# Strassen's scheme for part of the first up projection, with the S5 tables built in one batch

## The chip, the cores and the metric

The kernel runs on one core of one Trainium2 chip. The metric is the device time of one execution in microseconds (us). The kernel before takes 966.59 us, the median of 3 runs (966.46 to 968.69).

The core has a matrix engine (TensorE, PE in the profile, with its weight loads shown apart as PEld), VectorE (DVE), ScalarE (ACT), GpSimd (POOL), and SyncE (SP), whose queue issues nearly all DMA transfers here. Each engine works off its own queue in order.

## What the reference computes

One decoder layer on 512 tokens of width 1024, in float32, with adaLN shifts, scales and gates from a vector c:

```python
h = modulate(x, sh1, sc1)
x = layer_norm(ALPHA * x + 0.5 * g1 * swiglu(h, ffn1_w1, ffn1_w3, ffn1_w2), ...)
h = modulate(x, sh2, sc2)
m = hybrid_mixer(h, ...)          # Mamba-2 SSD heads and S5 heads, one shared w_in and w_out
x = layer_norm(ALPHA * x + g2 * m, ...)
h = modulate(x, sh3, sc3)
x = layer_norm(ALPHA * x + 0.5 * g3 * swiglu(h, ffn2_w1, ffn2_w3, ffn2_w2), ...)
# swiglu(u, w1, w3, w2) = (silu(u @ w1) * (u @ w3)) @ w2, inner width D_FF = 2816
# mod = (silu(c) @ w_ada + b_ada), nine chunks of 1024: shift, scale, gate three times
```

S5 is a complex diagonal state space with 32 groups of 64 states and 16 channels. Its discretised A, its B and its C depend on parameters only, not on the tokens.

## The kernel before, in words

**Arithmetic.** PE multiplies in the type fp32r. Each operand is split into a high part (a cast on ACT, `whi`) and the rest (a subtraction on DVE, `wlo`), and `mm3` (L101) makes each product of three matmuls: hi x hi, hi x lo, lo x hi.

**Stages.** The trace shows, in order: the first adaLN chunks with early pieces of the up projection (0 to 54 us), the first up projection (54 to 258), the first down projection (258 to 396), the mixer (396 to 607), the second up projection with its plain head (607 to 683) and its Strassen part (683 to 843), and the second down projection (843 to 967).

**Up projection.** The 2816 inner columns are 22 blocks f of 128. For each f, `up` (L397) multiplies the block of w1 (j = 0) and of w3 (j = 1) with all 512 tokens: 8 depth blocks x 3 matmuls of 512 columns each. `glue` (L384) then makes silu(a) * b on ACT and DVE into a tile `g`; the 22 blocks live in 11 `g` tiles. In the second projection `up_fast` (L477) takes the last 16 blocks by Strassen's scheme in Winograd's form: two blocks f, f+1 of one weight matrix form a 2 x 2 partition with the depth halves, the tokens another, and seven products replace eight. Each product is 4 depth blocks x 3 matmuls of 256 columns. A unit needs four sums of weights (L511, L512, L514, L522), all on DVE in before; the sums of the activations are made once by `h_sums` (L439).

**Side jobs.** Work that is not a projection is written as generators, and `step` (L609) advances them by a number of steps at places inside the projections. `s5_setup` (L775) builds, from parameters, four quarters b of tables: powers of A (`E`, seven doublings per real and imaginary part by `cmul`, six DVE operations each), the products `P0..P3` of B and `Q0..Q3` of C with powers of A. ACT copies P into block-diagonal tiles `bd` (L857), PE transposes them (L870) and multiplies them with `cd` (L901), and each quarter leaves for DRAM through tiles with tag `s5mp`, of which there are two (five uses a quarter, L872 to L919). The adaLN chunks are `ada_gate` (L302) and `ada_pair` (L283): each chunk is eight 512 KB loads into two `ra` buffers and eight DVE accumulates into `acc` (L276, L278). In `body` the side jobs of the first up projection are s5_setup with 4 steps per f, and from f = 11 the adaLN jobs with 3 steps per f; the down projection then advances the adaLN jobs by one step per f and half, and `L.step(ada, 1000)` finishes what is left:

```python
ada = [xres(), L.ada_gate(2, 0.5, g1), L.ada_pair(3, m2), L.ada_pair(6, m3), L.ada_gate(5, 1.0, g2)]
L.up(hT, gp, g, f0, jobs, 4, late=(ada, 3, 11), done=pss[f0, 0])
...
L.down(NF, getl_of(g, gl), L.make_drain(res, lambda: g1[0], ln1), 6, ada, 1)
L.step(ada, 1000)
```

xres yields 4 times, a gate 11 times (8 accumulates, 3 more), a pair 22 times.

**What sets the order.** The program is written once, engine by engine in the order of the calls; a scheduler then places the instructions in the engines' queues and may move ready work of ACT, DVE and the DMA queues ahead of work that comes earlier in the program. At run time each queue is strictly in order, and waits go by semaphores.

**Drains.** At the end of a down projection `make_drain` (L656) takes each of the four token tiles from PSUM: two or three DVE operations, bn_stats, a square root on POOL, the normalisation, and then `to_h` (L330) transposes it on PE and splits it for the next stage. The mixer begins with the z projection, whose weights are split as `zw`.

## Time and profile before

| | before |
|---|---|
| median of 3 runs | 966.59 us (966.46 to 968.69) |
| the profiled execution | 968.27 us, span 966.6 us |
| PE busy | 944.9 us, 5409 matmuls |
| DVE busy | 758.4 us, 1522 instructions |
| ACT busy | 446.9 us, 879 instructions |
| POOL busy | 34.2 us, 73 instructions |

The span is the time from the first to the last instruction of one profiled execution; 1.7 us of that execution's time lie around it. A share is busy time by span. The chain that ended last is followed back from the last instruction: at each step to what released it, or to the instruction before it on its engine; its shares say which engine's work the end depends on. Matmuls overlap in PE's pipeline, so the time of one is the distance from its start to the next one's, not the duration in its row.

### The profile page before, as it was taken

To read this page: it belongs to the slowest core of one execution; us is meant where nothing else is said; L and a number is where in the kernel's file an instruction comes from. 1 tells how busy PE (TensorE), PEld (TensorE's weight loads), DVE (VectorE), ACT (ScalarE), POOL (GpSimd) and SP (SyncE) were. 2 spreads that over 40 slices of the span, in tenths; PEclk is the share of its full clock that TensorE was granted. 3 is DMA by queue.
4 is the path that set the end of the run, shared out by engine and by line. 5 is a ranking of instruction groups with operands and counts; after the bars stand their busy time and mean duration, and the time that the engine had idled before them with its cause. 6 is when DMAs were issued, how large, how long until landed. Compare 5 with 4: busy or idle time off the path is not lost.

```text
span 966.6 us, 14710 instructions
## 1 busy us (share of the span) xinstructions
PE 944.9 (98%) x5409; PEld 798.1 (83%) x5409; DVE 758.4 (78%) x1522; ACT 446.9 (46%) x879; POOL 34.2 (4%) x73
## 2 busy tenths in 40 slices
...
GB/s 342 377 190 270 188 280 162 157 174 122 261 204 197 242 217 180 86 233 71 142 121 67 1 88 152 173 111 66 88 99 120 89 129 90 175 152 109 109 1 87
DMA packets 75578, 147.93 MB, mean 153 GB/s; under 512 B 11633, under 2 KB 28657, under 8 KB 74993
## 3 DMA queue, kind: packets, MB, share of 16 engines
...
q14 instruction: 32, 0.25, 0.1%
...
## 4 chain that ended last, share of the span: by engine, by line
PE 86%; DVE 6%; ACT 4%; issue 2%; POOL 1%; DMA 0%; DVEq 0%; POOLq 0%; ACTq 0%
PE ps L103 27%; PE ps L104 27%; PE ps L105 27%; DVE cv L90 1%; PE ps L253 1%; PE ps L978 1%; DVE wlo L81 1%; PE ps L207 1%; ACT whi L96 1%; POOL rsx L170 1%; DVE s5X L81 0%; DMA raw<-in_w_in_dram 0%; PE ps L295 0%; DVE s5t L81 0%; PE ps L949 0%
## 5 line engine op out<-in xcount | busy, mean ns | idle before, releaser
L96 ACT CAST whi<-raw 128x1024 fp32r<-128x1024 f32 (+1 forms) x155 | 155.0, 1007 | 211.5 <-PE ps L104 97.5
L81 DVE TENSOR_TENSOR wlo<-raw,whi 128x1024 fp32r<-128x1024 f32 (+1 forms) x155 | 179.3, 1167 | 43.0 <-ACT whi L96 42.5
L103 PE MATMUL ps<-hT,whi 128*128 128x512 f32 x448 | 177.0, 396 | 1.7 <-ACT hT L1492 1.7
L104 PE MATMUL ps<-hT,whi 128*128 128x512 f32 x448 | 174.7, 390 | 0.1
L105 PE MATMUL ps<-hT,wlo 128*128 128x512 f32 x448 | 174.6, 390 | 0.0
L103 PE MATMUL ps<-whi,ghl 128*128 128x512 f32 x320 | 125.2, 391 | 0.0
L104 PE MATMUL ps<-wlo,ghl 128*128 128x512 f32 x320 | 124.5, 389 | 0.0
L105 PE MATMUL ps<-whi,ghl 128*128 128x512 f32 x320 | 124.3, 389 | 0.0
L103 PEld LDWEIGHTS ps<-hT,whi 128*128 128x128 f32 x448 | 83.9, 188 | 23.3 <-issue 3.2
L105 PEld LDWEIGHTS ps<-hT,wlo 128*128 128x128 f32 x448 | 84.1, 188 | 17.8
L104 PEld LDWEIGHTS ps<-hT,whi 128*128 128x128 f32 x448 | 84.2, 188 | 17.0 <-DVE hT L81 0.5
L103 PE MATMUL ps<-hx,whi 128*128 128x256 f32 (+1 forms) x320 | 97.5, 305 | 0.7 <-DVE cp L90 0.6
L104 PE MATMUL ps<-hx,whi 128*128 128x256 f32 (+1 forms) x320 | 97.3, 304 | 0.0
L105 PE MATMUL ps<-hx,wlo 128*128 128x256 f32 (+1 forms) x320 | 97.3, 304 | 0.0
L90 DVE SCALAR_TENSOR_TENSOR acc<-ra,cs,acc 128x1024 f32<-128x1024 f32 (+2 forms) x62 | 71.0, 1145 | 22.4 <-DMA ra<-in_w_ada_dram 21.9
L96 ACT CAST ghl<-g 128x512 fp32r<-128x512 f32 x88 | 53.1, 619 | 50.1 <-PE ps L105 37.5
L103 PEld LDWEIGHTS ps<-whi,ghl 128*128 128x128 f32 x320 | 60.1, 188 | 14.6 <-issue 2.5
L105 PEld LDWEIGHTS ps<-whi,ghl 128*128 128x128 f32 x320 | 60.1, 188 | 12.6
L104 PEld LDWEIGHTS ps<-wlo,ghl 128*128 128x128 f32 x320 | 60.1, 188 | 12.3
L81 DVE TENSOR_TENSOR ghl<-g,ghl 128x512 fp32r<-128x512 f32 x88 | 58.1, 686 | 13.6 <-ACT ghl L96 13.6
L103 PEld LDWEIGHTS ps<-hx,whi 128*128 128x128 f32 x320 | 61.1, 191 | 3.9 <-issue 0.8
L104 PEld LDWEIGHTS ps<-hx,whi 128*128 128x128 f32 x320 | 61.2, 191 | 2.6
...
## 6 DMA issues: line engine op xcount, KB each, us to landing
ra<-in_w_ada_dram SPq DMA_DIRECT2D x56, 512.0 KB, 4.5
raw<-in_up_dram SPq DMA_DIRECT2D x49, 512.0 KB, 4.2
raw<-in_ffn_w_dram SPq DMA_DIRECT2D x44, 512.0 KB, 4.4
raw<-in_up_dram SPq DMA_DIRECT2D x64, 256.0 KB, 3.8
ra<-in_ada_dram SPq DMA_DIRECT2D x16, 512.0 KB, 7.8
raw<-in_w_in_dram SPq DMA_DIRECT2D x16, 512.0 KB, 4.4
s5d<-s5mp SPq DMA_DIRECT2D x20, 256.0 KB, 3.8
...
```

The lines of the kernel that those rows point to most:

```text
L81: self.nc.vector.tensor_tensor(out=out, in0=a, in1=b, op=op)
L90: self.nc.vector.scalar_tensor_tensor(out=out, in0=a, scalar=s, in1=b, op0=op0, op1=op1, **k)
L96: keep(self.nc.scalar.copy(out=hi, in_=src))
L103: mm(o, lh, rh, start=first, stop=False, **k)
L104: mm(o, lh, rl, start=False, stop=False, **k)
L105: self.last_mm = mm(o, ll, rh, start=False, stop=last, **k)
L170: self.nc.gpsimd.tensor_scalar(out=x, in0=var, scalar1=EPS, scalar2=None, op0=ADD)
L207: self.nc.tensor.matmul(ps, self.onesr, bc(self.onesr, (1, 4)), start=True, stop=True)
L253: nc.tensor.matmul(bank[q:q + 32, 0:256], lhs, w[:, :, m * P:(m + 1) * P], start=(j < 2), stop=(j >= len(put) - 2))
L978: nc.tensor.matmul(pv[32 * r:32 * r + 32, j, :], M[:, n, r, 32 * j:32 * j + 32], rhs[:, r, :], start=(n == 0), stop=(n == 2))
```

## The change

Four things change:

- The first up projection now takes its blocks f = 14 to 21 by `up_fast`, that is 8 units (4 pairs f, f+1, times j). Blocks 12 and 13 are plain and carry `h_sums`. In these units (add=True) two of the four weight sums are made by DMA transfers issued on POOL that add into their destination: one adds a weight block from DRAM to a raw tile just loaded, one adds a half of the sum tile `c` to a raw tile in SBUF.
- In the second up projection the plain head shrinks from 6 to 4 blocks (FAST 6 to 4), so 2 more units go by Strassen's scheme.
- `s5_setup` is batched: E is made in two halves of two quarters, with operations up to 512 wide, P and Q for all four quarters at once with 256-wide operations. Their scratch are the five last `g` tiles of the projection (`L.spare`). After that the four quarters' copies, transposes and transfers follow one another. It is stepped 6 times per f instead of 4.
- The adaLN jobs get 2 steps per f from f = 10 up to f = 11, then 2 steps per unit in `up_fast`, then one per f and half in the down projection, where the unfinished tail of `up_fast` (one step) stands ahead of them. The down projection's weights and those behind are put in the queue by `down1()` in the last unit.

```diff
-    def up_fast(self, hq, new, gp, gts, g, w, f0, last, jobs):
+    def up_fast(self, v, new, c, sp, gp, g, w, f0, last, jobs, per, add=False):
...
+            if add:
+                x = ts[0][:, 512:1024].rearrange("p (k n) -> p k n", k=4)
+                nc.gpsimd.dma_start(out=x, in_=w[f][:, j, 0:4], accum_op=ADD)
...
         def prep_a(u):
             a, b = raws[u]
-            self.tt(c[:, lo_], a[:, hi_], b[:, hi_], ADD)
-            self.tt(a[:, hi_], a[:, hi_], a[:, lo_], ADD)
+            if not add:
+                self.tt(c[:, lo_], a[:, hi_], b[:, hi_], ADD)
+                self.tt(a[:, hi_], a[:, hi_], a[:, lo_], ADD)
             split(u, a, ("b11", "t1"))
             self.tt(c[:, hi_], a[:, hi_], b[:, hi_], ADD)
+            if add:
+                self.tt(c[:, lo_], c[:, hi_], a[:, lo_], SUB)
 
         def prep_b(u):
-            split(u, raws[u][1], ("b21", "b22"))
+            b = raws[u][1]
+            split(u, b, ("b21", "b22"))
+            if add:
+                nc.gpsimd.dma_start(out=b[:, lo_], in_=c[:, hi_], accum_op=ADD)
 
         def prep_c(u):
             split(u, c, ("t3", "t2"))
-            b = raws[u][1]
-            self.tt(b[:, lo_], b[:, lo_], c[:, hi_], ADD)
+            if not add:
+                b = raws[u][1]
+                self.tt(b[:, lo_], b[:, lo_], c[:, hi_], ADD)
...
-            self.step(jobs, 1)
+            self.step(jobs, per)
...
-        E = (pt("Er", [P, 4, P]), pt("Ei", [P, 4, P]))
-        w3 = [P, 4, 16]
-        Pk = [(pt(f"p{k}r", w3), pt(f"p{k}i", w3)) for k in range(4)]
-        Qk = [(pt(f"q{k}r", w3), pt(f"q{k}i", w3)) for k in range(4)]
-        u1, u2 = pt("s5u1", w3), pt("s5u2", w3)
+
+        xt = big[4].rearrange("p a (q n) -> p a q n", n=64)
+        for h in range(2):
+            E = [big[2 * n + h].rearrange("p a (q t) -> p (a q) t", t=P) for n in range(2)]
+            q = slice(8 * h, 8 * h + 8)
+            nc.vector.memset(E[0][:, :, 0:1], 1.0)
+            nc.vector.memset(E[1][:, :, 0:1], 0.0)
+            for lg in range(7):
+                n = 1 << lg
+                er, ei = en[lg]
+                self.cmul(E[0][:, :, n:2 * n], E[1][:, :, n:2 * n], bc(er[:, q], (2, n)), bc(ei[:, q], (2, n)),
+                          E[0][:, :, 0:n], E[1][:, :, 0:n], xt[:, 0, :, :n], xt[:, 1, :, :n])
+                if lg in (3, 5):
+                    yield
+            for b in range(2):
+                for n in range(2):
+                    nc.sync.dma_start(out=self.s5_dram[2 * h + b][:, 2 + n], in_=E[n][:, 4 * b:4 * b + 4])
+            yield
+        v4 = lambda t: t.rearrange("p a (c q h) -> p (a c) q h", c=2, h=16)
+        PQ = [v4(t) for t in big[:4]]
+        Pk = [(PQ[k // 2][:, 2 * (k % 2)], PQ[k // 2][:, 2 * (k % 2) + 1]) for k in range(4)]
+        Qk = [(PQ[2 + k // 2][:, 2 * (k % 2)], PQ[2 + k // 2][:, 2 * (k % 2) + 1]) for k in range(4)]
+        u = v4(big[4])
+        u1, u2 = u[:, 0], u[:, 1]
+        wb = lambda a: bc(a, (2, 16))
+        self.cmul(*Pk[0], wb(fr), wb(fi), bt['s5_b_re'], bt['s5_b_im'], u1, u2)
+        yield
+        for k in (1, 2, 3):
+            self.cmul(*Pk[k], wb(A[k][0]), wb(A[k][1]), *Pk[0], u1, u2)
+            yield
+        for j in range(4):
+            self.cmul(*Qk[j], wb(A[j + 1][0]), wb(A[j + 1][1]), cb['s5_c_re'], cb['s5_c_im'], u1, u2)
+            yield
...
-            self.cmul(*Pk[0], wb(fr), wb(fi), bt['s5_b_re'][:, q], bt['s5_b_im'][:, q], u1, u2)
-            for k in (1, 2, 3):
-                if k == 2:
-                    yield
-                self.cmul(*Pk[k], wb(A[k][0]), wb(A[k][1]), *Pk[0], u1, u2)
...
-                        nc.scalar.copy(out=bd[n][sl, :, 3 - k, g, :], in_=Pk[k][n][sl])
+                        nc.scalar.copy(out=bd[n][sl, :, 3 - k, g, :], in_=Pk[k][n][sl, q])
...
-        FAST = 6
+        FAST1 = 14
+        FAST = 4
...
+        wsum = [L.gates.tile([P, 1024], F32, tag="gate", bufs=2, name="wsum1")]
+
+        def down1():
+            L.want_down(NF, ins['ffn1_w2'][0])
+            L.wlimit = len(L.wq)
+            L.want_mixer()
+            L.want_up(ins['up2'], (), HALVES, g_alloc, FAST)
+            L.wahead(L.wi + 2)
...
             L.glue(gp, g, f, pss[f, 0], pss[f, 1])
-        jobs = [L.s5_setup(pre)]
+        L.spare = [L.g_tile(gp) for _ in range(NF // 2 - (len(g) + 1) // 2)]
+        jobs = [L.s5_setup(pre, L.spare[-5:])]
         ada = [xres(), L.ada_gate(2, 0.5, g1), L.ada_pair(3, m2), L.ada_pair(6, m3), L.ada_gate(5, 1.0, g2)]
-        L.up(hT, gp, g, f0, jobs, 4, late=(ada, 3, 11), done=pss[f0, 0])
+        L.up(hT, gp, g, f0, jobs, 6, late=(ada, 2, 10), done=pss[f0, 0], nf=FAST1 - 2)
         L.step(jobs, 1000)
         pctx.close()
+        sctx = ExitStack()
+        sp = sctx.enter_context(tile_pool("f1"))
+        hs = [sp.tile([P, 2, 4, 2, P], F32R, tag="hs", bufs=3, name=f"hs1{k}") for k in range(3)]
+        quarter = lambda k, t: hT[:, 2 * t:2 * t + 2, 4 * k:4 * k + 4]
+        jobs = [L.h_sums(quarter, hs, L.spare[-3:])]
+        fast = L.up_fast(quarter, hs, wsum[0], sp, gp, g, ins['up1'], FAST1, down1, ada, 2, True)
+        lead = [(next(fast) for _ in range(4))]
+        L.up(hT, gp, g, FAST1 - 2, jobs, 4, late=(lead, 4, FAST1 - 1), nf=FAST1)
+        L.step(jobs, 1000)
+        L.step(lead, 4)
+        next(fast)
+        ada.insert(0, fast)
+        sctx.close()
...
-        L.up(hT3[0], fp, g, 0, jobs, 4, halves=HALVES, late=(lead, 4, FAST - 1), nf=FAST)
+        L.up(hT3[0], fp, g, 0, jobs, 5, halves=HALVES, late=(lead, 4, FAST - 1), nf=FAST)
```

`g_tile` hands out `L.spare` first and allocates a new tile when it is empty.

The queues at the places where instructions move, before and after. Names carry the program's numbers; the same f, j or chunk has another number in the two programs.

PE at the first S5 transposes, before: ps201 is one of the banks of f 8, bd0 and bd1 are the block-diagonal P of the first quarter.

```order
L104 MATMUL ps201_1346<-hT1_118,whi189_1219 128x512
L105 MATMUL ps201_1346<-hT1_118,wlo190_1220 128x512
L870 MATMUL ps202_1359<-ident_83,bd0_1179 128x128 x4
L870 MATMUL ps204_1367<-ident_83,bd1_1180 128x128 x4
L103 MATMUL ps201_1346<-hT1_118,whi189_1219 128x512
L104 MATMUL ps201_1346<-hT1_118,whi189_1219 128x512
L105 MATMUL ps201_1346<-hT1_118,wlo190_1220 128x512
```

The transposes stand in the middle of a bank's products. The same place after: ps208 is the bank of f 8, j = 1, ps219 that of f 9, j = 0.

```order
L105 MATMUL ps208_1430<-hT1_119,whi196_1309 128x512
L106 MATMUL ps208_1430<-hT1_119,wlo197_1310 128x512
L895 MATMUL ps209_1443<-ident_83,bd0_1110 128x128 x4
L895 MATMUL ps211_1451<-ident_83,bd1_1111 128x128 x4
L104 MATMUL ps219_1502<-hT1_119,whi201_1361 128x512
L105 MATMUL ps219_1502<-hT1_119,whi201_1361 128x512
L106 MATMUL ps219_1502<-hT1_119,wlo202_1362 128x512
```

The transposes now stand between the last product of f 8 and the first of f 9.

DVE at this place, before: g183 is the glue of a block f, wlo199 a weight split, s5x, s5u, Er and Ei belong to one quarter.

```order
L81 TENSOR_TENSOR q3i_1204<-s5u1_1205,s5u2_1206 128x64
L81 TENSOR_TENSOR Er_1187<-s5x214_1446,s5x215_1447 128x4x4
L81 TENSOR_TENSOR gs298_2200<-acc258_1850,gs297_2199 128x1024
L81 TENSOR_TENSOR g183_1082<-sl193_1262,ps192_1225 128x512
L81 TENSOR_TENSOR wlo199_1341<-raw191_1223,whi198_1340 128x1024
L81 TENSOR_TENSOR s5x214_1446<-e2r_1090,Ei_1188 128x4x4
L81 TENSOR_TENSOR s5x215_1447<-e2i_1091,Er_1187 128x4x4
L81 TENSOR_TENSOR s5u1_1205<-s5fr_1003,s5_b_re_683 128x64
L81 TENSOR_TENSOR Ei_1188<-s5x214_1446,s5x215_1447 128x4x4
L81 TENSOR_TENSOR s5u2_1206<-s5fi_1004,s5_b_im_686 128x64
L81 TENSOR_TENSOR s5x214_1446<-e3r_1092,Er_1187 128x4x8
```

Behind a glue and a split stand operations of 16 to 64 columns. DVE after, from the glue of f 8 on: g135 to g139 are the five scratch tiles (E real and imaginary of both halves, and a temporary), ps208 is the bank above.

```order
L82 TENSOR_TENSOR g133_667<-sl213_1471,ps208_1430 128x512
L82 TENSOR_TENSOR g137_671<-g139_673 128x8x32
L82 TENSOR_TENSOR wlo224_1578<-raw207_1428,whi223_1577 128x1024
L82 TENSOR_TENSOR g139_673<-e6r_1041,g135_669 128x512
L82 TENSOR_TENSOR g139_673<-e6i_1042,g137_671 128x512
L82 TENSOR_TENSOR g135_669<-g139_673 128x8x64
L82 TENSOR_TENSOR g139_673<-e6r_1041,g137_671 128x512
L82 TENSOR_TENSOR g139_673<-e6i_1042,g135_669 128x512
L82 TENSOR_TENSOR g137_671<-g139_673 128x8x64
L82 TENSOR_TENSOR g139_673<-e0r_1029,g136_670 128x8
L82 TENSOR_TENSOR g139_673<-e0i_1030,g138_672 128x8
L82 TENSOR_TENSOR g136_670<-g139_673 128x8
```

Behind the last row shown, 39 more operations finish E's second half, 24 of 128x256 make P (into g135 and g136), and 24 make Q. ACT's copies into bd0 and bd1 read all four P.

PE at the start of the mixer, before: res1 is the second token tile, zw the split weights of the z projection.

```order
L339 MATMUL ps583_3986<-ident_83,res1_121 128x128 x4
L339 MATMUL ps584_3997<-ident_83,res1_121 128x128 x4
L103 MATMUL ps601_4059<-zw589_4024,hT2_2995 128x512
L104 MATMUL ps601_4059<-zw589_4024,hT2_2995 128x512
L105 MATMUL ps601_4059<-zw589_4024,hT2_2995 128x512
L103 MATMUL ps601_4059<-zw589_4024,hT2_2995 128x512
```

After, with modsb of adaLN chunks 6 and 7, and gs, the split accumulator of the gate of chunk 5:

```order
L340 MATMUL ps600_4178<-ident_83,res1_122 128x128 x4
L221 MATMUL ps605_4200<-ident_83,modsb568_3988 128x128 x4
L319 MATMUL ps619_4239<-gs617_4235,onesr_90 128x512
L319 MATMUL ps620_4243<-gs617_4235,onesr_90 128x512
L320 MATMUL ps619_4239<-gs618_4236,onesr_90 128x512
L320 MATMUL ps620_4243<-gs618_4236,onesr_90 128x512
L104 MATMUL ps633_4287<-zw621_4252,hT2_3169 128x512
L105 MATMUL ps633_4287<-zw621_4252,hT2_3169 128x512
L106 MATMUL ps633_4287<-zw621_4252,hT2_3169 128x512
```

The gate's four matmuls stood inside the down projection before, and stand now between the last transposes and the z projection.

DVE at the same place, after: hT2 is the mixer's input, acc608 the accumulator of chunk 5.

```order
L82 TENSOR_TENSOR hT2_3169<-tf598_4166,hT2_3169 128x4x128
L86 TENSOR_SCALAR modc606_4205<-modc606_4205 128x8
L91 SCALAR_TENSOR_TENSOR acc608_4210<-ra616_4232,cs_98,acc608_4210 128x1024
L82 TENSOR_TENSOR G885_6079<-cols_639,modc606_4205 128x8
L82 TENSOR_TENSOR B886_6080<-cols_639,modc606_4205 128x8
L82 TENSOR_TENSOR hT2_3169<-tf598_4166,hT2_3169 128x4x128
L82 TENSOR_TENSOR B886_6080<-B886_6080,modc606_4205 128x8
L86 TENSOR_SCALAR gate943_6599<-gate943_6599 128x1024
L82 TENSOR_TENSOR gs618_4236<-acc608_4210,gs617_4235 128x1024
L91 SCALAR_TENSOR_TENSOR gate607_4208<-ps619_4239,gate607_4208 128x512
L91 SCALAR_TENSOR_TENSOR gate607_4208<-ps620_4243,gate607_4208 128x512
L82 TENSOR_TENSOR zw621_4252<-raw566_3969,zw621_4252 128x1024
```

The last accumulate, the split of the gate and its two reads of PSUM stand ahead of the first z weight. The seven other accumulates of acc608 stand between the drains of the four token tiles; in before all eight, and the z weights too, stand ahead of the first drain.

## Rows read from the trace of the kernel before

**Rows 1.** The page: busy us, share, instructions; shares of the chain.

```profile
PE 944.9 (98%) x5409; PEld 798.1 (83%) x5409; DVE 758.4 (78%) x1522; ACT 446.9 (46%) x879; POOL 34.2 (4%) x73
...
PE 86%; DVE 6%; ACT 4%; issue 2%; POOL 1%; DMA 0%; DVEq 0%; POOLq 0%; ACTq 0%
```

**Rows 2.** Stretches: length, busy us of PE, PEld, DVE, ACT, POOL; clock, DMA.

```profile
54.00:258.00 204.00, 204.00 (x960) 166.70 (x963) 163.72 (x653) 90.20 (x247) 6.33 (x12) 1.00 0.62 203
...
396.00:607.00 211.00, 202.24 (x1308) 163.37 (x1306) 171.97 (x277) 124.42 (x266) 14.94 (x36) 0.98 0.32 106
...
683.00:843.00 160.00, 159.30 (x1305) 157.95 (x1305) 135.17 (x199) 87.55 (x144) 0.00 (x0) 1.00 0.34 111
```

**Rows 3.** Timeline, PE, plain projection: start us, duration us, line, names, shape.

```profile
150.23 0.39 PE L103 MATMUL ps<-hT,whi 128*128 128x512 f32 x1
...
150.91 0.39 PE L103 MATMUL ps<-hT,whi 128*128 128x512 f32 x1
```

**Rows 4.** Timeline, PE, Strassen part of the second projection.

```profile
690.21 0.28 PE L103 MATMUL ps<-hx,whi 128*128 128x256 f32 x1
...
690.81 0.28 PE L105 MATMUL ps<-hx,wlo 128*128 128x256 f32 x1
```

**Rows 5.** Timeline, PE, first S5 transposes.

```profile
115.71 1.03 PE L870 MATMUL ps<-ident,bd 128*128 128x128 f32 x8
```

**Rows 6.** Timeline, DVE, first up projection.

```profile
112.73 1.22 DVE L81 TENSOR_TENSOR wlo<-raw,whi 128x1024 fp32r<-128x1024 f32 x1
113.86 0.17 DVE L81 TENSOR_TENSOR s5x<-e2r,Ei 128x16 f32<-128x16 f32 x1
113.95 0.17 DVE L81 TENSOR_TENSOR s5x<-e2i,Er 128x16 f32<-128x16 f32 x1
...
120.32 0.42 DVE L81 TENSOR_TENSOR s5x<-e6r,Er 128x256 f32<-128x256 f32 x1
120.66 0.42 DVE L81 TENSOR_TENSOR s5x<-e6i,Ei 128x256 f32<-128x256 f32 x1
```

**Rows 7.** Timeline, DVE, end of the first down projection.

```profile
375.53 1.29 DVE L90 SCALAR_TENSOR_TENSOR gate<-ps,gate 128x512 f32<-128x512 f32 x2 [0.29 <-PE ps L319]
...
383.08 0.68 DVE L81 TENSOR_TENSOR dr<-ps,gate 128x512 f32<-128x512 f32 x1
383.68 0.21 DVE L81 TENSOR_TENSOR wdtr<-wdt,wdtr 128x64 fp32r<-128x64 f32 x1
```

**Rows 8.** Instructions on s5mp: durations ns min/median/max, first and last start.

```profile
L915 ACT COPY s5mp<-ps x40: 254/258/262, 139.6 to 264.1; 32x128 f32<-32x128 f32 x40
L90 DVE SCALAR_TENSOR_TENSOR s5mp<-ident,s5par,s5mp x16: 343/346/351, 146.9 to 265.2; 128x128 f32<-128x128 f32 x16
L872 ACT COPY s5mp<-ps x8: 585/592/595, 116.3 to 237.7; 128x512 f32<-128x512 f32 x8
...
L877 POOL MEMSET s5mp<- x8: 524/527/531, 123.4 to 241.3; 128x512 f32 x8
...
L881 ACT ACTIVATE s5mp<-q1r x8: 236/238/242, 124.1 to 242.1; 64x64 f32<-64x64 f32 x8
...
DMA to landing us min/median/max: 2.0/3.8/6.3
```

**Rows 9.** Groups by form: busy us, mean ns; idle before, releaser.

```profile
L90 DVE SCALAR_TENSOR_TENSOR acc<-ra,cs,acc 128x1024 f32<-128x1024 f32 x49 | 62.8, 1282 | 22.1 <-DMA ra<-in_w_ada_dram 21.9
```

**Rows 10.** The page's DMA issues: count, KB each, median us to landing.

```profile
ra<-in_w_ada_dram SPq DMA_DIRECT2D x56, 512.0 KB, 4.5
...
raw<-in_up_dram SPq DMA_DIRECT2D x64, 256.0 KB, 3.8
ra<-in_ada_dram SPq DMA_DIRECT2D x16, 512.0 KB, 7.8
```

**Rows 11.** Timeline, PE, first z matmuls; in brackets the idle time before.

```profile
399.39 0.62 PE L105 MATMUL ps<-zw,hT 128*128 128x512 f32 x1 [1.14 <-DVE hT L81]
...
403.14 0.39 PE L105 MATMUL ps<-zw,hT 128*128 128x512 f32 x1
```

58 lines of the change are left out of this document (18 added, 40 removed).

## The prediction

> **What bounds the kernel now.** I read the page's busy shares and its chain first, then the stage table, then the timelines of TensorE (PE) and VectorE (DVE) at the places where the new order differs. PE is busy 98% of the span and is 86% of the chain that ends last; DVE is busy 78% and is only 6% of the chain [rows 1]. The stage table shows where there is room: in the first up projection (54 to 258 us) PE is busy 204.00 of 204.00 us with DVE at 163.7; in the mixer (396 to 607) PE loses 8.8 of 211 us; in the Strassen stage of the second up projection (683 to 843) PE loses 0.7 of 160 [rows 2]. So whatever shortens PE's work counts in full, and whatever makes PE wait in the first up projection costs in full, since nothing waits there now.
>
> **Gain on PE.** A plain pair of blocks, one weight matrix, is 2 x 8 x 3 = 48 matmuls of 512 columns. From 150.23 to 150.91 three of them start, 0.227 us each [rows 3]: 10.88 us. The Strassen unit that replaces it is 7 products x 4 x 3 = 84 matmuls of 256 columns; from 690.21 to 690.81 five start, 0.120 us each [rows 4]: 10.08 us. Ten more units (8 in the first projection, 2 in the second) give 10 x 0.80 = 8.0 us. The DVE side of a unit (splits, sums, glue) fits under it: the Strassen stage has DVE at 135 of 160 us with PE at 159.3 [rows 2], and the new units have two sums fewer on DVE. I count it as hidden; uncovered, it would cost at most some tenths a unit, as in that stage now (0.7 us over 16).
>
> **Cost A: S5 setup in one block, in front of f 9.** Before, each of the four S5 quarters comes by itself, with 64-wide operations between weight splits, and its eight transposes cost PE 1.03 us in the middle of a bank [rows 5]. After, all of P and Q are computed at once, and the first quarter's transposes need the last of P. On PE they stand directly behind f 8's last matmul and ahead of f 9 (first order fence). On DVE the glue of f 8 reads the bank of that last matmul; behind the glue in the same queue stand a weight split, the last step of E's first half, all 42 operations of its second half, and the 24 operations of P. All of them start only when PE has already run out of allowed work. Their price, start to start: 16-wide 0.09, 256-wide 0.34, 1024-wide 1.13 us [rows 6], 512-wide 0.60 (383.08 to 383.68) [rows 7], that is 0.07 + columns/960. So:
> - glue 0.60, one 256-wide 0.34, split 1.13: 2.1 us;
> - six operations of 512: 3.6 us;
> - six each of 8, 16, 32, 64, 128, 256 and 512 columns: 6 x 1.55 = 9.3 us;
> - P, 24 of 256: 8.1 us.
>
> That is 23.1 us. To it come the ScalarE (ACT) copies of the last P into bd (some four of 0.25 us by the like copies of Q [rows 8]) and waits between dependent operations. DVE also comes late to the glue: eight adaLN accumulates at 1.28 us each [rows 9] now stand just ahead of it, two buffers deep, each pair waiting for a 512 KB load of 4.5 us [rows 10]. I put these three together at 0 to 8 us and take 2. PE idle: 25 us, bounds 21 (the wide operations a little cheaper than the rule) and 31.
>
> After the nearest wait in this trace, 1.1 us at the mixer's start, nine matmuls of 512 columns start in 3.75 us (399.39 to 403.14), 0.42 each instead of 0.227, which is the pace of the lower of the clock's two levels, 1.2 GHz: 1.7 us lost [rows 11]. I add 2 once, bounds 1 and 4.
>
> **Cost B: S5's four quarters in a row, f 9 to f 12.** A quarter now has about one f of PE time, not the 40 us between quarters of before (the POOL memsets run from 123.4 to 241.3 us in four groups [rows 8]). It passes five tiles through two buffers (tag s5mp). Filling: two by one copy of 0.59; two by a memset of 0.53 and four copies of 0.24 (1.5 each); one by a memset, ten copies of 0.26 and four DVE operations of 0.35 (4.5): 8.7 us. Each then leaves by a 3.8 us transfer: 5 x 3.8 = 19 [rows 8]. So (8.7 + 19) / 2 = 13.9 us a quarter, against 10.88 for f and about 1.9 for 17 small matmuls, 12.8. PE's queue holds the next quarter's transposes ahead of the next f, so a late buffer reaches PE: 4 x 1.1 = 4.4 us, and the first quarter starts with ACT behind. I take 6, bounds 0 and 15.
>
> **Cost C: the start of the mixer.** The adaLN steps are counted out by the code: 4 + 11 + 22 + 22 + 11 = 70 are needed. Before gives 11 x 3 in the up projection and 44 in the down projection, 77, so the last gate (chunk 5) is finished inside it, at 375.53, before the drains begin at 383.08 [rows 7]. After gives 2 x 2, then 8 x 2, then 43: 63. The last seven steps fall to the end of the down projection, and DVE's queue shows it (last order fence): the eight accumulates of that gate stand between the drains of the four token tiles, and the split of the gate (gs), its two PSUM reads and only then the z-weight splits (zw) come behind the last drain. On PE the gate's matmuls stand ahead of the z projection, which in before began its run at 399.39 [rows 11]. Summing DVE's queue by the prices above from the last ghl split (376.1 us in before) to the first zw: 7 x 1.2 + 0.66 for the accumulates, 1.1 + 1.2 for gs and the gate, 0.7, 1.1 for zw, and 15.3 for the drains and normalised tiles, 28.5 us, so 404.6 at the earliest, 5 us late. The accumulates' loads, two at a time at 4.5 us, and POOL's square root in each drain add up to 8. I take 10 us, bounds 5 and 13. The low clock after this wait is paid in before too.
>
> **The adding DMAs** (two per unit, issued by POOL) aren't in the trace. The one into b has about five of a unit's seven products between its issue and the split that reads it, at 10.08 / 7 each some 7 us; the one into a, issued with the load a unit and more ahead, has more. Nearest rows: 256 KB loads land in 3.8 us, the slowest group in 7.8 [rows 10]. I take 0, bounds 0 and 8 (eight units x about 1 us). The Trainium skill, SBUF — State Buffer, "Who interferes with whom", says that a DMA held up by a DVE operation is one whose descriptors GpSimd writes, GpSimd having to wait for the port that it shares with DVE; no run here shows it, and it speaks against these transfers. By the skill's DMA: Bandwidth & Descriptors, "Anatomy of one DMA", the fit for this path gives an estimate of 2.6 us for 256 KB, and the sum would be the same.
>
> **Sum.** -8 + 25 + 2 + 6 + 10 = +35 us on the profiled execution's 968.27 (span 966.6 and 1.7 around it): 1003 us. That execution lies 1.7 above the median of 966.59, so I predict 1002 us. With all lower bounds: -8 + 21 + 1 + 0 + 5 = +19, 985; all upper: -8 + 31 + 4 + 15 + 13 + 8 = +63, 1030.
>
> **Rivals.**
> 1. Faster, 959 us: S5's block stays hidden behind f 8, as all of S5 is now (PE 204.00 of 204.00 [rows 2]), and the accumulates stay hidden at the mixer. Then only the 8.0 us remain. It decides at the glue of f 8: if DVE has E and P behind it when PE ends f 8, this is it; the break-even is a wait of 8 us in all. For it: DVE has 40 us to spare in that stage. Against: the glue stands ahead of 73 operations and waits for PE's last allowed matmul.
> 2. Only A: the tail of S5 and the gate run in slack, for ACT is 44% busy in the up stage [rows 2] and the drains have POOL gaps that accumulates can fill. 966.6 - 8 + 27 = 986 us.
> 3. The adding DMAs land late in each unit: at 7.8 us and more, with POOL's order behind them, 3 to 5 us of PE wait in each of 8 units on top of the forecast, 1026 to 1042 us. By the rule of the SBUF page above it would be this one.
> 4. The wait pays back: while PE stands still, loads and splits run ahead, and part of the mixer's 8.8 us of idle time goes. 1002 - 8 = 994 us, inside my range.
>
> **How the numbers follow.** Forecast (with rival 4) 0.77; rival 2 0.09; rival 3 0.07; rival 1 0.05; something that ends within 0.3% (2.9 us, about what a measurement of this kernel can tell from no change) 0.02. The range 984 to 1022 holds the forecast's own bounds but for their far upper end, and rival 2; left out are rival 1, rival 3 and that end, under 2 in 10. Faster 0.05, same 0.03, slower 0.92.
>
> **What would show it.** In the changed kernel's profile: one PE idle of 20 to 30 us near 116 us that ends at the L895 transposes, with DVE full of 256- and 512-wide operations on g tiles in it; smaller PE waits at L895 or for s5mp in the four f behind; PE's L104 on zw some 10 us later after the last drain than now, released by gs; Strassen units of 10.1 us in the first projection, without a wait for POOL's DMAs. Wrong would be: no idle over 5 us near 116 us (rival 1), or idle of several us in each of the 8 units (rival 3).

## The result, and the profile after

The changed kernel takes 1026.29 us (median of 4 runs, 1025.37 to 1028.5) against 967.37 for the kernel before in the same job: ratio 1.0608 [1.0594, 1.0623], 59 us slower. Forecast were 1002 us and 984 to 1022. Each forecast cost is there, at its place; the sum was 24 us short. The page of the changed kernel, against [rows 1]:

```profile
PE 944.4 (92%) x5769; PEld 812.2 (79%) x5769; DVE 800.2 (78%) x1381; ACT 479.1 (47%) x938; POOL 48.4 (5%) x89
...
PE 64%; DVE 16%; DMA 8%; ACT 5%; issue 4%; POOL 1%; SPq 0%; DVEq 0%; POOLq 0%; ACTq 0%
```

PE's idle time (span less busy) is 1024.3 - 944.4 = 79.9 us; before it was 966.6 - 944.9 = 21.7. So 58.2 us of new waits make up all of the 57.7 us of span. PE's busy time is the same, though the ten units saved some 8: the lower clock took that back (mean granted clock 0.967, before 0.995). The stages, against [rows 2]; up projection, down projection, mixer, second head, second Strassen part:

```profile
54.00:316.00 262.00, 214.45 (x1302) 188.00 (x1302) 193.52 (x495) 122.10 (x310) 20.51 (x28) 0.92 0.56 168
316.00:454.00 138.00, 128.26 (x570) 101.89 (x568) 110.66 (x148) 53.19 (x81) 3.60 (x10) 0.98 0.62 197
454.00:665.00 211.00, 202.23 (x1293) 162.61 (x1292) 171.90 (x268) 125.55 (x264) 12.62 (x30) 0.97 0.37 118
665.00:714.00 49.00, 48.69 (x316) 44.23 (x315) 42.89 (x55) 20.74 (x35) 1.99 (x3) 1.00 0.41 129
714.00:896.00 182.00, 181.39 (x1508) 181.05 (x1507) 153.43 (x224) 96.24 (x155) 0.00 (x0) 1.00 0.33 106
```

The up projection lost 47.6 us of PE time and the end of the down projection 9.7; the second projection runs as forecast. PE's timeline at the first S5 transposes, which in before stood in the stream without a wait [rows 5], and behind them:

```profile
117.98 0.39 PE L106 MATMUL ps<-hT,wlo 128*128 128x512 f32 x1
155.07 1.09 PE L895 MATMUL ps<-ident,bd 128*128 128x128 f32 x4 [36.71 <-ACT bd L888]
156.33 1.09 PE L895 MATMUL ps<-ident,bd 128*128 128x128 f32 x4 [0.17 <-ACT bd L888]
157.06 0.77 PE L104 MATMUL ps<-hT,whi 128*128 128x512 f32 x1
157.64 0.63 PE L105 MATMUL ps<-hT,whi 128*128 128x512 f32 x1
158.06 0.63 PE L106 MATMUL ps<-hT,wlo 128*128 128x512 f32 x1
```

That is wait A: 36.7 us, forecast 25. DVE's timeline in it (from 118.36 PE stands still):

```profile
121.73 1.28 DVE L91 SCALAR_TENSOR_TENSOR acc<-ra,cs,acc 128x1024 f32<-128x1024 f32 x1 [0.57 <-DMA ra<-in_w_ada_dram]
122.94 0.42 DVE L82 TENSOR_TENSOR g<-g 128x256 f32<-128x256 f32 x1
124.83 1.28 DVE L91 SCALAR_TENSOR_TENSOR acc<-ra,cs,acc 128x1024 f32<-128x1024 f32 x1 [1.48 <-DMA ra<-in_w_ada_dram]
...
126.70 0.68 DVE L82 TENSOR_TENSOR g<-sl,ps 128x512 f32<-128x512 f32 x1
...
153.97 0.42 DVE L82 TENSOR_TENSOR g<-g 128x256 f32<-128x256 f32 x1
```

The glue of f 8 starts at 126.70, 8.3 us after PE stopped. The last real part of P ends at 153.97 + 0.42 = 154.39, 27.7 us on, and 0.7 us of ACT copies end the wait: 8.3 + 27.7 + 0.7 = 36.7. The accumulates ahead of the glue, and what the wide operations cost:

```profile
L91 DVE SCALAR_TENSOR_TENSOR acc<-ra,cs,acc 128x1024 f32<-128x1024 f32 x14 | 17.9, 1281 | 3.8 <-DMA ra<-in_w_ada_dram 3.8
...
145.65 0.42 DVE L82 TENSOR_TENSOR g<-s5fr,s_b_re 128x256 f32<-128x256 f32 x1
145.99 0.42 DVE L82 TENSOR_TENSOR g<-s5fi,s_b_im 128x256 f32<-128x256 f32 x1
146.45 0.42 DVE L82 TENSOR_TENSOR g<-g 128x256 f32<-128x256 f32 x1
146.91 0.42 DVE L82 TENSOR_TENSOR g<-s5fr,s_b_im 128x256 f32<-128x256 f32 x1
```

The first line is the group by form from 54 to 155.7 us; twelve of the fourteen start by 118.4 us, where before has seven of this form. In the other lines, the second product starts 0.34 us after the first, as in [rows 6], but their difference, which reads it, 0.46 us later, and the product that overwrites what the difference reads 0.46 later again. In before, another job's operations stood between such pairs.

Waits B, at the transposes of the second and third quarter: PE, and what ACT did ahead of the first of them:

```profile
185.21 0.66 PE L895 MATMUL ps<-ident,bd 128*128 128x128 f32 x4 [3.90 <-ACT bd L888]
201.72 0.66 PE L895 MATMUL ps<-ident,bd 128*128 128x128 f32 x4 [2.81 <-ACT bd L888]
...
182.06 2.68 ACT L927 COPY s5mp<-ps 32x128 f32<-32x128 f32 x10
184.77 0.39 ACT L888 COPY bd<-g 64x64 f32<-64x64 f32 x2
```

The last two copies into bd stand in ACT's queue behind ten copies of the quarter before. A third wait, 0.99 us, follows at 208.29 on k.

Wait C, PE at the start of the mixer, against 1.14 us in [rows 11]:

```profile
453.31 1.22 PE L319 MATMUL ps<-gs,onesr 128*128 128x512 f32 x2 [8.76 <-ACT gs L97]
...
458.11 0.79 PE L105 MATMUL ps<-zw,hT 128*128 128x512 f32 x1 [1.66 <-DVE zw L82]
```

And the adding DMAs, from the page, with who waited for the second (the tile wsum, in the units):

```profile
raw<-in_up_dram POOLq DMA_DIRECT2D x8, 256.0 KB, 3.7
raw<-wsum POOLq DMA_DIRECT2D x8, 256.0 KB, 3.7
...
ACT whi L97: 12.6, 5
DVE wsum L82: 11.3, 5
```

### The profile page after: what moved, and what is told of

Read it like the earlier page. It is cut to its first block, busy times and chain, and to the rows that moved or that the text cites. A ratio compares the mean times of both kernels' runs of the same rounds, so it can differ in the third digit from the quotient of the medians.

```text
span 1024.3 us, 15479 instructions
## 1 busy us (share of the span) xinstructions
PE 944.4 (92%) x5769; PEld 812.2 (79%) x5769; DVE 800.2 (78%) x1381; ACT 479.1 (47%) x938; POOL 48.4 (5%) x89
## 4 chain that ended last, share of the span: by engine, by line
PE 64%; DVE 16%; DMA 8%; ACT 5%; issue 4%; POOL 1%; SPq 0%; DVEq 0%; POOLq 0%; ACTq 0%
PE ps L104 20%; PE ps L105 20%; PE ps L106 20%; DVE g L82 3%; DMA ra<-in_w_ada_dram 2%; DVE wlo L82 2%; DMA raw<-wsum 2%; DVE acc L91 2%; DMA raw<-in_up_dram 1%; DVE s5t L82 1%; DMA s5d<-s5mp 1%; ACT whi L97 1%; DMA ew<-in_up_dram 1%; DVE cv L91 1%; ACT s5mp L927 1%
## 5 line engine op out<-in xcount | busy, mean ns | idle before, releaser
L97 ACT CAST whi<-raw 128x1024 fp32r<-128x1024 f32 (+1 forms) x165 | 161.0, 983 | 206.0 <-PE ps L106 73.1
L82 DVE TENSOR_TENSOR wlo<-raw,whi 128x1024 fp32r<-128x1024 f32 (+1 forms) x165 | 186.2, 1139 | 45.4 <-ACT whi L97 45.2
L104 PE MATMUL ps<-hT,whi 128*128 128x512 f32 (+1 forms) x448 | 165.0, 370 | 3.0 <-ACT hT L1509 2.4
L105 PE MATMUL ps<-hT,whi 128*128 128x512 f32 (+1 forms) x448 | 162.7, 363 | 0.1
L106 PE MATMUL ps<-hT,wlo 128*128 128x512 f32 (+1 forms) x448 | 162.4, 362 | 0.0
L104 PE MATMUL ps<-whi,ghl 128*128 128x512 f32 x320 | 125.2, 391 | 0.0
L106 PE MATMUL ps<-whi,ghl 128*128 128x512 f32 x320 | 124.2, 389 | 0.0
L104 PEld LDWEIGHTS ps<-hT,whi 128*128 128x128 f32 x448 | 85.5, 191 | 19.1 <-issue 3.8
L106 PEld LDWEIGHTS ps<-hT,wlo 128*128 128x128 f32 x448 | 85.5, 191 | 13.1
L105 PEld LDWEIGHTS ps<-hT,whi 128*128 128x128 f32 x448 | 85.7, 191 | 12.5 <-DVE hT L82 0.5
L104 PE MATMUL ps<-hx,whi 128*128 128x256 f32 (+1 forms) x320 | 94.0, 294 | 0.6 <-DVE cp L91 0.6
L105 PE MATMUL ps<-hx,whi 128*128 128x256 f32 (+1 forms) x320 | 94.0, 294 | 0.0
L106 PE MATMUL ps<-hx,wlo 128*128 128x256 f32 (+1 forms) x320 | 93.9, 294 | 0.0
L104 PE MATMUL ps<-hs,whi 128*128 128x256 f32 x312 | 88.6, 284 | 2.4 <-ACT cp L586 2.4
L105 PE MATMUL ps<-hs,whi 128*128 128x256 f32 x312 | 88.3, 283 | 0.0
L106 PE MATMUL ps<-hs,wlo 128*128 128x256 f32 x312 | 88.3, 283 | 0.0
L104 PEld LDWEIGHTS ps<-whi,ghl 128*128 128x128 f32 x320 | 60.1, 188 | 15.6 <-ACT ghl L97 3.4
L106 PEld LDWEIGHTS ps<-whi,ghl 128*128 128x128 f32 x320 | 60.1, 188 | 12.5
```

The lines of the kernel that those rows point to most:

```text
L82: self.nc.vector.tensor_tensor(out=out, in0=a, in1=b, op=op)
L97: keep(self.nc.scalar.copy(out=hi, in_=src))
L104: mm(o, lh, rh, start=first, stop=False, **k)
L105: mm(o, lh, rl, start=False, stop=False, **k)
L106: self.last_mm = mm(o, ll, rh, start=False, stop=last, **k)
```

## The experiments

Each ratio is to the kernel before, with its 95% interval. "First wait" is PE's idle ahead of the first S5 transposes.

### What made the first wait long

**e5_batch_alone**: the kernel before with the batched setup alone.

```diff
-        FAST1 = 14
-        FAST = 4
+        FAST1 = 22        # no Strassen unit in the first projection
+        FAST = 6
...
```

> The kernel before with the batched S5 setup alone (6 steps per f): no new Strassen units, no adding DMAs, adaLN jobs as before. Theory (the wait for the last of P, A, and the row of quarters, B, come from the batch itself, not from the Strassen units): PE idle of 25 to 37 us at the first S5 transposes, some 5 to 8 us in the quarters behind, no wait at the mixer, no 8.0 us gain: 1000 to 1014 us. Rival (in the changed kernel the wait is that long because adaLN accumulates and the work of the units crowd VectorE): a wait under 15 us, 970 to 985 us.

Measured: 1.0472 [1.0439, 1.0504], 1011.8 us; first wait 37.73, two of 3.62 and 1.97 in the quarters, nothing at the mixer. The rival falls: neither the units nor the adding DMAs are needed for waits A and B.

**e1_ada_inorder**: the adaLN accumulates of the first up projection stay at their place in the program (keep tells the scheduler so).

```diff
-                self.stt(acc, w, s, acc, MUL, ADD)
+                keep(nc.vector.scalar_tensor_tensor(out=acc, in0=w, scalar=s, in1=acc, op0=MUL, op1=ADD))
...
```

> The changed kernel with the adaLN accumulates of the first up projection kept in program order on DVE, so none of them stands ahead of f 9; nothing else moves by hand. Theory (the wait of 36.7 us at the first S5 transposes is DVE arriving 8.3 us late at the glue of f 8, because of 16 accumulates pulled ahead, plus 28.4 us of E and P behind that glue): without the accumulates DVE has done E and part of P before the glue, about 18 operations of 256 columns at 0.42 us and one split are left, so the wait falls to 8 to 12 us and the time to 998 to 1004. Rival (the batch itself is too long for DVE wherever the accumulates stand): the wait stays at 25 us or more, 1013 or more. Second rival: the accumulates are now late and the mixer's start waits longer than 11 us, which gives part of it back.

Measured: 1.0521 [1.0505, 1.0536], 1017.7 us. First wait 14.37 instead of 36.71, so 22.3 of it were accumulates moved ahead and what they waited for. But only 8.6 us of time were won: thirteen of them come between 133 and 306 us instead, and PE then waits in the quarters (9.3 us) and the units (about 10). So time is given back as the second rival says, but not at the mixer's start that it named, where the waits are those of the changed kernel (8.75 and 1.66). PE and DVE at the first transposes:

```profile
124.19 0.68 DVE L83 TENSOR_TENSOR g<-sl,ps 128x512 f32<-128x512 f32 x1
...
133.16 1.09 PE L897 MATMUL ps<-ident,bd 128*128 128x128 f32 x4 [14.37 <-ACT bd L890]
```

The first line is the glue of f 8: it now stands in the middle of P, and all of E is done ahead of it.

**e7_four_temps**: the complex products without dependent neighbours.

```diff
-            self.cmul(*Pk[k], wb(A[k][0]), wb(A[k][1]), *Pk[0], u1, u2)   # mul mul sub, mul mul add
+            cm(Pk[k], A[k], Pk[0])     # four muls into four temporaries, then sub, add
...
```

> The changed kernel with each complex product of E (all but the widest doubling) and of P and Q made of four products into four temporaries and then the two sums, so that an operation seldom reads what the one just before it wrote. The same operations, the same widths. Theory: behind the glue of f 8 about 20 triples of operations stand that now take 0.25 us each longer than the distance of independent ones (1.26 against 1.01 us for 256 columns); the wait of 36.7 us shortens by 4 to 5 us, to about 32, and the time by as much, 1021 to 1022 us. Rival (the distance belongs to the scattered operands, not to the dependence): wait and time unchanged, 1025 to 1027 us.

Measured: 1.0471 [1.0457, 1.0485], 1012.9 us, 13.4 less than the changed kernel; first wait 24.60. DVE's timeline shows the step of 0.34 throughout (x2 is a difference and a sum):

```profile
134.67 0.42 DVE L82 TENSOR_TENSOR g<-s5fr,s_b_re 128x256 f32<-128x256 f32 x1
135.01 0.42 DVE L82 TENSOR_TENSOR g<-s5fi,s_b_im 128x256 f32<-128x256 f32 x1
135.34 0.42 DVE L82 TENSOR_TENSOR g<-s5fr,s_b_im 128x256 f32<-128x256 f32 x1
135.68 0.42 DVE L82 TENSOR_TENSOR g<-s5fi,s_b_re 128x256 f32<-128x256 f32 x1
136.01 0.75 DVE L82 TENSOR_TENSOR g<-g 128x256 f32<-128x256 f32 x2
...
L91 DVE SCALAR_TENSOR_TENSOR acc<-ra,cs,acc 128x1024 f32<-128x1024 f32 x10 | 12.8, 1282 | 1.2 <-DMA ra<-in_w_ada_dram 1.1
```

The dependence is real, and the effect over twice the forecast, because the first half of E gains too and four accumulates fewer (17.9 - 12.8 = 5.1 us) come ahead of P. That the scheduler moves fewer ahead, and puts E's second half ahead of the glue of f 8 (which starts at 128.14), are side effects, so the 12.1 us aren't all dependence.

**e11_both**: the edits of e1 and e7 together, no others.

> The changed kernel with both edits that shortened the first wait: adaLN accumulates in program order through the first up projection, and complex products into four temporaries. Up to the last operation of P, VectorE's queue in the changed kernel holds 16 accumulates of 18.1 us, and 35.2 us of wide S5 operations that took 26.8 with four temporaries. Theory (VectorE has work all the time from 54 us to the last of P, so the wait is what is left of this sum when PE ends f 8): 36.7 - 22.3 - 8.4 - about 1 = 4 to 6 us at the first transposes, and about 1008 us, since the accumulates return later as they did with program order alone. Rival (the two shorten the same stretch and don't add): 10 to 14 us.

Measured: 1.0458 [1.0444, 1.0471], 1011.6 us; first wait 6.96, a little above the 4 to 6 of the theory and well under the rival's 10. The two add up nearly in full, and the rest returns in the quarters and the units, as in e1.

### Whether other orders avoid the waits

**e2_E_behind**: E made after the four quarters, with six empty steps ahead of them.

```diff
+        for _ in range(6):
+            yield
         mpart = lambda: pre.tile([P, 4, P], F32, tag="s5mp", bufs=2, name=self.nm("s5mp"))
...
+        xt = big[4].rearrange("p a (q n) -> p a q n", n=64)
+        for h in range(2):
...
```

> The changed kernel with the powers E computed after the four S5 quarters instead of before P and Q (six empty steps keep the quarters at their place). Accumulates are pulled ahead as in the changed kernel. Theory (the transposes need only P; what makes them late is that E, 84 operations, stands ahead of P in DVE's queue): P is ready before f 8 ends, the wait of 36.7 us falls under 3 us, the time to 986 to 993. Rival (the accumulates, not E, make DVE late): a wait of 8 us or more stays, 998 or more.

Measured: 1.0386 [1.0367, 1.0404], 1005.4 us. The theory is right at the place and wrong on the time: the first wait is gone, but a new one of 15.28 us stands at the first Strassen unit (PE L104 on hs), because E works in the g tiles that `h_sums` needs next.

**e6_old_s5**: the setup of before, stepped so that it ends in time.

```diff
-        jobs = [L.s5_setup(pre, L.spare[-5:])]
+        jobs = [L.s5_setup(pre)]
-        L.up(hT, gp, g, f0, jobs, 6, late=(ada, 2, 10), done=pss[f0, 0], nf=FAST1 - 2)
+        L.up(hT, gp, g, f0, jobs, 8, late=(ada, 2, 10), done=pss[f0, 0], nf=FAST1 - 2)
```

> The changed kernel with the S5 setup of before (each quarter by itself, tables in small tiles of its own), stepped 8 times per f so that it ends before the Strassen units. Theory: no wait at the first transposes; the wait at the mixer's start (8.8 + 1.7 us) stays, 10 units give 8.0 us; so 968 - 8 + 12 = 972 us, up to 980 with small waits in the plain blocks, where VectorE has more to do in fewer blocks. Rival (the narrow operations of the old setup don't fit into 8 blocks of f fewer): VectorE late by several us in each quarter, 990 us and more.

Measured: 1.0463 [1.0429, 1.0497], 1011.3 us: the rival. Two waits of 9.55 and 11.02 us stand at the first and the last quarter's transposes: the setup that was hidden with 40 us a quarter isn't hidden with 22 to 33. So going back to the old setup doesn't take the waits away either. Whether S5's own work or the accumulates beside it (six, 7.7 us, in DVE's queue from 54 to 100 us) make DVE late there is not separated by this run.

**c3_E_quarter**: P and Q in a batch, E by quarters, beside each quarter.

```diff
-        for h in range(2):          # E for two quarters at once, ahead of P
+            powers(b, range(5))     # E of quarter b, inside quarter b, in tiles of its own
...
```

> The changed kernel with P and Q batched as they are, but E made quarter by quarter in small tiles of its own beside the transposes of its quarter, and 6 empty steps between Q and the first quarter. Theory: what PE waits for at the first transposes is the DVE work in front of P; with E gone from there and six steps of room the wait is under 3 us, the quarters cost 5 to 8 us as now, the mixer's wait stays at 10.4: 968 - 8 + 12 + 6 = 978 us, 972 to 985. Rival (any removal of the wait is given back behind it, as in the run with accumulates in program order): 995 us and more.

Measured: 1.0407 [1.0387, 1.0426], 1006.5 us: no first wait, but 12.43 at hs, since the last quarter's E stands ahead of `h_sums` in DVE's queue. The rival holds.

**c4_E_quarter_ada**: the same with the adaLN steps earlier.

```diff
-        L.up(hT, gp, g, f0, jobs, 6, late=(ada, 2, 10), done=pss[f0, 0], nf=FAST1 - 2)
+        L.up(hT, gp, g, f0, jobs, 6, late=(ada, 3, 9), done=pss[f0, 0], nf=FAST1 - 2)
-        lead = [(next(fast) for _ in range(4))]
+        lead = [((next(fast), L.step(ada, 1)) for _ in range(4))]
...
```

> As the run with E by quarters, and with the adaLN steps moved earlier: 3 per f from f 9 on, one more with each of the four lead steps of the Strassen units, and the residual load without steps of its own. Theory: the last gate is then finished inside the down projection, the wait at the mixer (8.8 + 1.7 us) goes, and 965 to 972 us are left, near the time before. Rival (the plain blocks have no VectorE time left for the earlier accumulates, their waits come in the up projection): the same total as with E by quarters or more, 978 to 990 us.

Measured: 1.0285 [1.0264, 1.0306], 995.5 us, 11.0 less than c3 and above the numbers of both theory and rival. The theory is right on wait C, which is gone (1.14 us at L106 on zw, as before): from the first matmul of the down projection to the third of the z projection c3 takes 142.7 us, c4 128.3; 5.7 of that are given back in the up projection, where hs still waits 10.23. The changed kernel takes 143.0 us for this stretch, the one before 129.8.

**e3_ada3**: more adaLN steps in the units alone.

```diff
-        fast = L.up_fast(quarter, hs, wsum[0], sp, gp, g, ins['up1'], FAST1, down1, ada, 2, True)
+        fast = L.up_fast(quarter, hs, wsum[0], sp, gp, g, ins['up1'], FAST1, down1, ada, 3, True)
```

> The changed kernel with 3 adaLN steps per Strassen unit in the first projection instead of 2, so that 71 of the 70 needed steps are given before the mixer. Theory (the 10.4 us idle around the gate's matmuls before the z projection come from the last gate falling behind the drains): that idle goes back to the 1.9 us of the kernel before, time 1014 to 1018. Rival (DVE's drains and not the gate set the start): under 4 us gained. Second rival: eight more accumulates in the Strassen units make DVE late there and cost 5 us or more of what is gained.

Measured: 1.0664 [1.0643, 1.0685], 1032.3 us: the second rival. C shrank to 3.86 + 2.67 + 1.66 us only, and a wait of 8.16 came in the last unit, where DVE was late from accumulates that waited for their loads.

**e4_mp4**: more s5mp buffers.

```diff
-        mpart = lambda: pre.tile([P, 4, P], F32, tag="s5mp", bufs=2, name=self.nm("s5mp"))
+        mpart = lambda: pre.tile([P, 4, P], F32, tag="s5mp", bufs=4, name=self.nm("s5mp"))
```

> The changed kernel with four s5mp buffers instead of two. Theory (the three waits of 3.9, 2.8 and 1.0 us at the transposes of the later quarters come from five tiles of a quarter passing two buffers): they fall under 2 us together, with the low clock behind them 8 to 10 us less, 1016 to 1018. Rival (ACT's own work for a quarter, about 10 us, sets the pace): they stay above 5 us, 1024 to 1027.

Measured: 1.0593 [1.0569, 1.0617], 1025.3 us, the same: the waits in the quarters are 1.8 + 5.8 instead of 3.9 + 2.8 + 1.0. Two more buffers don't take B away, as the rival says and as the rows of B above suggest; but ahead of the 5.8 ACT still sits idle for 2.93 us until a tile of s5mp is free.

### The adding DMAs

**e12_dve_sums** and **e13_add** start Strassen at f 16 and spread the S5 work (below); they differ in the last argument, True for the adding DMAs:

```diff
-L.up_fast(quarter, hs, wsum[0], sp, gp, g, ins['up1'], FAST1, down1, ada, 2, True)
+L.up_fast(quarter, hs, wsum[0], sp, gp, g, ins['up1'], FAST1, down1, ada, 2)
```

> As the run with Strassen from f 16 on, with products into four temporaries, three s5mp buffers instead of two, and all four sums of weights on VectorE (no adding DMAs). Theory: the waits of 2.4 and 4.5 us in the quarters go with the buffers and the shorter products, those of 1.1 and 3.8 us in the units with the adding DMAs, and the low clock behind them; 977 - 12 = 962 to 967 us, at or below the kernel before. Rival (VectorE, with two sums more a unit, is late in the units instead): 970 us and more.

> The same kernel as the one with all sums on VectorE, but with the adding DMAs kept. Theory (the sum tile that VectorE makes next waits for the second adding DMA to have read it, and this lands late): waits of 2 to 5 us in all inside the units, 3 to 6 us slower than with all sums on VectorE. Rival (the adding DMAs are hidden, or worth it for the two sums they take off VectorE): the same time or faster than with all sums on VectorE.

Measured: e12 0.9988 [0.9978, 0.9999], 966.3 us; e13 1.0081 [1.0064, 1.0098], 975.3 us: the adding DMAs cost 9 us in six units. Windows of the units, first e12 and then e13:

```profile
210.00:271.40 61.40, 61.40 (x502) 59.46 (x501) 53.50 (x75) 32.23 (x52) 0.00 (x0) 1.00 0.53 175
```

```profile
210.00:281.70 71.70, 64.06 (x508) 61.62 (x507) 50.26 (x69) 31.82 (x53) 6.93 (x8) 0.95 0.61 182
```

With all sums on it DVE is busy 53.5 of 61.4 us, and PE never waits. PE's waits of 2.85 (e12) and 2.68 us (e13) in the quarters are alike. The wait in e13's units, by DVE's, POOL's, ACT's and PE's timelines:

```profile
241.30 1.22 DVE L82 TENSOR_TENSOR wlo<-raw,whi 128x1024 fp32r<-128x1024 f32 x1
...
246.84 0.86 POOL L498 DMA_DIRECT2D raw<-in_up_dram  x1 [13.34 <-DMA raw<-in_up_dram]
247.78 0.87 POOL L526 DMA_DIRECT2D raw<-wsum  x1
...
254.75 0.62 ACT L97 CAST whi<-raw 128x512 fp32r<-128x512 f32 x1 [9.75 <-DMA raw<-wsum]
255.27 0.38 ACT L549 ACTIVATE g<-ps 128x256 f32<-128x256 f32 x1
255.55 0.36 ACT L586 COPY cp<-ps 128x256 f32<-128x256 f32 x1
...
255.96 0.58 PE L104 MATMUL ps<-hs,whi 128*128 128x256 f32 x1 [7.04 <-ACT cp L586]
```

POOL's queue holds the next unit's first adding DMA (L498), which waits for the load that it adds to; the urgent one (L526) is issued right behind it, at 247.78. What it adds to was read for the last time by the split that ends at 242.52, so POOL's order held it up for 5.3 us. It then took 6.9 us to land, where the median of the five in these units is 4.1. ACT's cast of its result then holds the copy that PE's next product needs. The theory's wait is there too (DVE's next sum waits 3.34 us for the same transfer, up to 254.67), but the one that reaches PE goes by ACT, and the cost is above the theory's 3 to 6 us. The waits of this kind are 1.06 and 3.76 in e9 and 0.73 and 1.64 in the changed kernel.

**e15_sums_alone**: the same edit, and nothing else, in the changed kernel.

> The changed kernel with all four sums of weights on VectorE in the first projection as in the second, so without the adding DMAs; all else as changed. Theory (POOL issues the second adding DMA behind the first one of the next unit, which waits for a load; ScalarE's cast of its result then holds the copies that free PE's banks): the waits of 0.7 and 1.6 us in the units go with the low clock behind them, so 3 us less than the changed kernel, 1023 us (ratio 1.056 to 1.059). Rival (VectorE is the engine that is short, and two sums more a unit make it late): the same as the changed kernel or slower, 1026 us and more.

Measured: 1.0530 [1.0516, 1.0545], 1019.5 us, 6.8 less than the changed kernel. That is more than the theory's 3 us. From the units' first matmul to the first of the down projection it is 82.4 us instead of 85.4; the waits of 0.73 and 1.64 are gone, and one of 0.6 at the last product stays in both. Between the two profiled executions, 1020.50 and 1026.06 us, 1.1 us more are at A and B and 0.7 at the mixer's start; what is left of the 6.8 isn't explained.

### A version that is faster

**e8_second_only**: in the kernel before, the second projection's part alone.

```diff
-        FAST = 6
+        FAST = 4
-        L.up(hT3[0], fp, g, 0, jobs, 4, halves=HALVES, late=(lead, 4, FAST - 1), nf=FAST)
+        L.up(hT3[0], fp, g, 0, jobs, 5, halves=HALVES, late=(lead, 4, FAST - 1), nf=FAST)
```

> The kernel before with only the plain head of the second up projection cut from 6 to 4 blocks, so two more Strassen units there, with nothing else changed. Theory: two units at 0.80 us, 1.6 us less, 966.4 against 968.0 us (ratio 0.998). Rival (the shorter head leaves too little time for the sums of the activations and the first weight splits): no change or some us slower, ratio 1.000 to 1.005.

Measured: 1.0025 [1.0013, 1.0036], 970.8 us: the rival, a quarter of a per cent slower. The last gate's split and four sums of a unit stand together in DVE's queue, and PE waits once for 2.04 us (L103 on whi at 720.81), with the low clock behind. In the changed kernel, where that wait is absent, the two units do bring their gain: the head takes 49.2 instead of 70.5 us, the Strassen part and its two units more 181.7 instead of 161.9 us, sum -1.5.

**e14_f14_spread**: c4 with four temporaries, three s5mp buffers, all sums on DVE, and E spread:

```diff
+        for b in range(2):          # ahead of the first quarter
+            powers(b, range(5))
+            yield
+            powers(b, range(5, 7))
+            yield
...
+            if b < 2:               # in the first two quarters
+                powers(b + 2, range(5))
```

> Strassen from f 14 on as in the change (8 units), with P and Q batched in the g tiles, E quarter by quarter spread ahead of and beside the first two quarters, four temporaries, three s5mp buffers, earlier adaLN steps and all sums on VectorE. Theory (VectorE's amount of work before f 14 is the limit, and two blocks fewer can't hold it): waits of 10 us and more in the up projection, 975 to 985 us, slower than Strassen from f 16 on. Rival (the order alone was at fault): under 5 us of waits, 960 to 966 us.

Measured: 1.0078 [1.0063, 1.0093], 974.7 us; waits of 9.3 us in the quarters, and 86.6 us for the eight units, counted as in e15, which takes 82.4 (waits of 1.0 and 1.5, and eight adaLN matmuls among them). This is just outside the theory's numbers and far from the rival's. But it doesn't show that there is too much work ahead of f 14. All of the 9.3 us stand at the transpose of k, where e12, with the same three buffers, has an empty step more and no wait. Ahead of the longest, ACT is not busy: it waits for a tile of s5mp, and POOL's memset of this tile for the transfer before:

```profile
122.65 0.52 POOL L916 MEMSET s5mp<- 128x512 f32 x1 [119.36 <-DMA s5d<-s5mp]
...
123.21 1.39 ACT L920 ACTIVATE s5mp<-g 64x64 f32<-64x64 f32 x8 [6.00 <-POOL s5mp L916]
...
125.57 0.26 ACT L933 COPY k<-ps 128x128 f32<-128x128 f32 x1
...
125.89 0.48 PE L936 MATMUL ps<-ident,k 128*128 128x128 f32 x1 [5.35 <-ACT k L933]
```

Strassen from f 14 on with these empty steps, or with more buffers, was not run.

**e9_f16**: Strassen from f 16 on; E spread as in e14, adaLN steps early as in c4 (from f 10), two empty steps ahead of the first quarter and two more in each, P0 and P1 in a tile outside the g tiles.

```diff
-        FAST1 = 14
+        FAST1 = 16
-        jobs = [L.s5_setup(pre, L.spare[-5:])]
+        jobs = [L.s5_setup(pre, [pre.tile([P, 2, S], F32, name="pq0")] + L.spare[-4:])]
...
```

> Strassen from f 16 on instead of f 14 (6 units in the first projection instead of 8); P and Q batched, their first tile outside the g tiles; E quarter by quarter, two quarters ahead of the first transposes and two beside the first two quarters; two empty steps more in each quarter; adaLN steps earlier, as in the run with earlier adaLN steps. Theory (the waits come from too little program order between VectorE's or ScalarE's work and the PE instruction that needs it, so two more blocks of f relieve them): the waits in the quarters fall under 5 us and the one for the sums of the activations under 2, so 968 - 6.4 + 3 to 8 = 965 to 972 us. Rival (VectorE's amount of work in the first projection is the limit, whatever the order): 980 us and more.

Measured: 1.0099 [1.0084, 1.0115], 977.0 us: between the two, with 8 us of waits in the plain blocks and 5 for the adding DMAs. e12, above, is this kernel with four temporaries, three s5mp buffers and all sums on DVE.

**e10_f16_inorder**: e9 with keep of e1 up to the end of S5, no other edit.

> As the run with Strassen from f 16 on, and the adaLN accumulates kept in program order until the S5 setup has ended. Theory (the accumulates that move ahead are what makes VectorE late for the first quarters): waits in the up projection under 5 us in all, 962 to 968 us. Rival (what is not done early comes back behind f 14, as it did in the run with accumulates in program order): 5 us or more above the run with Strassen from f 16 on.

Measured: 1.0114 [1.0099, 1.0129], 978.3 us, the same as e9 within the intervals: waits of 2.02 and 6.00 us in the quarters and 4.1 in the units. Neither holds; with two blocks more, the order of the accumulates no longer decides.

**e16_room**: e12 with one step more between ACT's copies into bd and their transposes, and without the two empty steps ahead of the first quarter.

```diff
-        for _ in range(2):
-            yield
...
             yield
+            yield
             for n in range(2):
                 ps = self.bank([P, 4, P])
```

> The fastest version (Strassen from f 16 on, all sums on VectorE, four temporaries) with the two empty steps ahead of the first quarter moved into the quarters: one step more between ScalarE's copies into bd and the transposes that read them, in each of the four quarters. Theory (the 2.9 us wait comes from copies that stand too close ahead of the transposes): the wait falls under 1 us, 962 to 965 us. Rival (S5 then ends later, or the first quarter gets late for want of the two steps): waits elsewhere, 966 us and more.

Measured: 963.86 us (963.43 to 966.27, 5 runs), ratio 0.9965 [0.9952, 0.9978], 4 us (0.35%) under the kernel before: the fastest version, and the theory's time. The longest wait between 54 us and the end of its up projection is 0.93 us. The page:

```profile
PE 936.2 (97%) x5697; PEld 803.9 (84%) x5697; DVE 797.2 (83%) x1466; ACT 472.3 (49%) x927; POOL 34.1 (4%) x73
```

PE has 8.7 us less to do than before, of which the eight units are 6.4, and idles 961.8 - 936.2 = 25.6 us against 21.7.

## Why the prediction was wrong, point by point

- **The bound** was read rightly: PE's waits in the first up projection cost in full, and they are nearly all of the difference.
- **The gain, -8.0**: right per unit. In e15 the eight units take 82.4 us; without the wait of 0.6 and the four gate matmuls among them (0.9) that is 10.1 a unit. In the changed kernel the gain is invisible, since PE's busy time didn't fall. Behind wait A, with PE idle for 36.7 us, the granted clock from 155.0 to 158.5 us is 0.50, and a matmul takes 0.42 us (157.64 to 158.06 above) instead of 0.227 [rows 3]: the lower of the two levels. "2 us of low clock, once", in bounds of 1 and 4, was 7.5 by difference (944.4 - 944.9 + 8.0), since there were several waits.
- **Cost A, the failed step: 25 put, 36.7 measured.** Its mechanism, place and order were as written; the term that was mis-sized is the one that put ACT's copies, the waits between dependent operations and DVE's coming late to the glue together at 2, in 0 to 8. They measure 0.7, 5.6 and 8.3, together 14.6. With the 22.1 us that the prediction's prices give up to the last real part of P this is 36.7. DVE came late because the prediction saw the eight accumulates ahead of the glue, but did not add up DVE's queue from 54 us on, where twelve accumulates stand by 118.4 us instead of seven, beside the first half of E. e1 shows what the accumulates are worth: 22.3 us of the wait, for without them E's second half is done ahead of the glue too. The 5.6 are 27.7 less 22.1: the prices came from independent neighbours, and two waits of 0.12 in each of 23 triples (two products and their sum or difference) make 5.5. e7 and e11 bear this out.
- **Cost B, 6**: 7.7 measured (3.90 + 2.81 + 0.99), inside its bounds. The prediction laid it to the two buffers; four of them don't shorten it (e4), and the rows of B show ACT's own copies ahead of the last copies into bd. In another version one step more between these copies and the transposes removes such a wait (e16); in the changed kernel this was not tried.
- **Cost C, 10**: 8.76 + 1.66 us where before had 0.7 + 1.1, so 8.5 more; the stretch around it takes 143.0 - 129.8 = 13.2 us more, with the smaller waits and the low clock in it. Right in kind (c4 removes it), and about its size. The sum for it starts 0.6 us early: the last ghl split of before begins at 376.74, not at 376.1.
- **The adding DMAs, 0 in 0 to 8**: 2.4 us of waits in the units, 6.8 by e15. Rival 3 had the mechanism (POOL's order behind a late transfer), but named 24 to 40 us; that the total, 1026 us, lies at the lower end of its 1026 to 1042 is chance. The Trainium skill, SBUF — State Buffer, "Who interferes with whom", says that a DMA held up by a DVE operation is one whose descriptors GpSimd writes. The rows here name a load and the order of POOL's queue instead, and no run here tests the port.
- **Rival 4**, the pay-back: no; the mixer's start has 8.5 us more of waits, not fewer.

With the measured terms, -8 + 36.7 + 7.5 + 7.7 + 8.5 (C less the 1.9 us that before had there) + 2.4 = 54.8 of the 57.7 us; the rest are waits of up to 0.7 us, at the start and in the drains above all. The prediction's own sum of upper bounds, 1030 us, holds the result; but cost A and the low clock went beyond their upper bounds (31 and 4), while C and the adding DMAs stayed under theirs.
